# Modulation products of a two-block transformer kernel spread anew over its stages; two small elementwise steps moved from VectorE to ScalarE

## The chip, the cores and the metric

One Trainium2 chip (trn2); the kernel runs on one of its cores. The metric is device time in microseconds (us) of one execution. The kernel before took 1667.27 us, the median of three runs (1662.65 to 1669.86).

## The reference, cut to what matters

Two transformer stacks follow each other on 256 tokens of width 1024. The first has two layers (three mixing branches, a gated feed-forward, a per-layer gate). The second takes its result as `x` (the "latent" stream), has a second stream `ctx` of 256 tokens, and modulates each norm by vectors that depend on a conditioning vector alone:

```python
s_lat = silu(c); s_ctx = silu(c_ctx)
for i in range(2):                       # layer 0: pooling, layer 1: attention
    sh1, sc1, g1, sh2, sc2, g2 = split(s_lat @ ada_w[i] + ada_b[i], 6)   # 1024 -> 6 * 1024
    a_l = rms_norm(h_lat) * (1 + sc1) + sh1
    # the same with s_ctx for ctx: csh1 ... cg2 in layer 0, csh1 and csc1 alone in layer 1
    h_lat = h_lat + g1 * mixer(a_l)
    m_l = rms_norm(h_lat) * (1 + sc2) + sh2
    h_lat = h_lat + g2 * (square(relu(m_l @ mlp_w1[i])) @ mlp_w2[i])
return rms_norm(h_lat)
```

The products `s @ ada_w[i]` depend on nothing else in the program. They can be made at any time before the first use of the part concerned. In the order of their 6144 columns the parts are shift, scale, gate of the first norm, then shift, scale, gate of the second.

## The kernel before

All weights but the modulation's are read from memory once, in chunks of eight 128x128 blocks (512 KB), in an order that the function `_plan` writes out. A class `Stream` works along this list. For each chunk it issues the load into one of four `raw` buffers (L326, on SyncE's queue), makes a rounded copy `hi` on ScalarE (L368) and the remainder `lo = raw - hi` on VectorE (L377), each with five buffers. Each block is then three matmuls on TensorE: `hi` with the activations' high part (L563), `hi` with their low part (L564), `lo` with the high part (L565). A chunk is so 24 matmuls of 256 columns for one set of activations. The function `linear` runs one matrix this way: at each chunk's start it takes the next chunk and lets every background generator in `bg` make one step (`bg_step`), and after the chunk's last matmul it calls `chunk_end`.

All engines run their instructions in the order in which the Python code records them. So the place of a call in the code is the place of its instructions in each engine's queue.

The modulation matrices are 48 chunks each (`ada0`, `ada1`). `_plan` puts an `ada` chunk behind a weight chunk whenever a sum of shares (the argument `share` of `add`) reaches one. An `ada` chunk is not split. It is loaded to one of two buffers of its own, and VectorE multiplies it with the conditioning vector and sums over the row (L578, tile `aprod`): twice for the 48 chunks of `ada0` and the first 16 of `ada1` (latent and context stream), once for the other 32, so 160 products in all. `chunk_end` makes all products of an `ada` chunk at once:

```python
def ada_chunk():
    ...
    for v in range(2 if i == 0 or c < 16 else 1):
        V.scalar_tensor_tensor(out=aprod, in0=w, scalar=1.0, in1=cvec[:, v], ...)
```

When all 48 chunks are done, `mod_cols(i, c)` adds the bias and makes the gains; it is called in the feed-forward of the first stack's second layer for i = 0 and after `m101` for i = 1.

The stages, in order, are named by their weights, with the layer's number at the end. First stack: `u`, `ug`, `kr`, `fq`, `fk`, `fv` (projections), `ga`, `gc`, `uq`, `uk`, `uv`, `brc`, `bra`, `gb`, `brb` (gates and branches, with the two attentions in between), `wo`, `ff` (44 chunks), `dn`, `pl`, `pg`. Second stack: `m100`, `m200`, `m100` and `m200` again (the first half of the MLP, for context and latent), `m101` (both streams at once, so 48 matmuls to a chunk), `m201` twice, then layer 1's `k`, `v`, `q`, `awo`, `m110` to `m211`.

Three more places matter. `per_layer` (stage `pg`) takes each pair of output columns out of PSUM on VectorE (L1245), runs a tanh on ScalarE, and in a background step updates `x` on VectorE (L1250, L1251), splits it for the next layer (L707 on ScalarE, L711 on VectorE) and sums its squares for the norm (L663, L667); the next stage `u1` needs the split in its third and fourth chunks and the sums at its 22nd block (L673). `Attention.norms` scales the probabilities on VectorE (L775, L777) before TensorE transposes them (L783). `ev1` squares relu's result on VectorE (L1467).

Of the kernel before, what the change touches and what calls it, by code (L numbers as in the profile page):

```python
# [258 lines left out]
def _plan(nblocks):  # L259

    plan = []

    adas = [(f"ada{i}", c) for i in range(DEPTH) for c in range(48)]
    due = [0]

    def add(name, first=0, last=None, share=0):

        nb = nblocks[name]
        for c in range(first, -(-nb // CB) if last is None else last):
            plan.append((name, c, min(CB, nb - c * CB)))  # L270
# [18 lines left out]
    add("m200", 0, LATA, 0.3)  # L289
    add("pool")  # L290
    add("m200", LATA, None, 0.3)
    add("m100", share=0.3)
    add("m200", share=0.3)
    add("m101", share=0.9)
    for n in ("m201", "m201", "k", "v", "k"):
        add(n)
    add("q", 0, QA)
    add("v")
    add("q", QA)
    for n in ("awo", "m110", "m111", "m210", "m211"):  # L300
        add(n)
    assert not adas
    return plan

# [110 lines left out]
def body(ctx: ExitStack, tc: tile.TileContext, dram, outT):  # L415
# [156 lines left out]

    def ada_chunk():
        name, c, _ = plan[st.pos]
        i = int(name[3])
        w = st.get(name, c)
        for v in range(2 if i == 0 or c < 16 else 1):
            V.scalar_tensor_tensor(out=aprod, in0=w, scalar=1.0, in1=cvec[:, v], op0=ALU.mult, op1=ALU.mult,  # L578
                                   accum_out=ada[:, i, v, c:c + 1])
        ada_done[i] += 1  # L580
# [159 lines left out]
    class Attention:  # L740
# [520 lines left out]

    def mod_cols(i, c):

        assert ada_done[i] == 48
        used = 48 if i == 0 or c == 0 else 16
        V.tensor_tensor(out=ada[:, i, c, 0:used], in0=ada[:, i, c, 0:used], in1=pc(f"adab{i}", 0, used), op=ALU.add)
        for n in range(used // 24 if used == 48 else 1):
            sc = ada[:, i, c, 8 + 24 * n:16 + 24 * n]
            V.scalar_tensor_tensor(out=modg[:, i, c, n, :], in0=sc, scalar=1.0, in1=pc(f"ng{i}{n}"), op0=ALU.add, op1=ALU.mult)
        if i == 0:  # L1270
            V.tensor_tensor(out=gps[:, c], in0=ada[:, 0, c, 16:24], in1=pc("ps"), op=ALU.mult)
# [545 lines left out]
```

## Time and profile before

| | us |
|---|---|
| median of three runs (lowest, highest) | 1667.27 (1662.65, 1669.86) |
| the profiled execution's own time | 1675.58 |
| its span, first to last instruction | 1673.8 |
| TensorE matmuls busy in the span | 1622.0 (97%) |
| VectorE busy | 1326.3 (79%) |
| ScalarE busy | 886.7 (53%) |
| GpSimd busy | 127.0 (8%) |

Busy times are sums over the span and say nothing of a single stage. Matmuls overlap in the records, so TensorE's busy share hides short stalls; a stage's length against a like stage's shows them.

### The profile page before, as it was taken

Reading aid. Unit: us, or ns where it says so; the run is one execution under the profiler, and the core shown is the slowest. Engines: PE = TensorE matmul, PEld = TensorE weight load, DVE = VectorE, ACT = ScalarE, POOL = GpSimd, SP = SyncE. Lnnn points to the kernel's source line nnn. Section 1 sums busy time; section 2 is a strip of 40 time slices with the busy share of each in tenths; the row PEclk is TensorE's granted clock in tenths of the full one; section 3 lists DMA queues with packets and bytes.
Section 4 is the critical chain, followed back from the end, with each engine's and each line's share of the span. In section 5 each row is a group of like instructions: output and inputs, shape, how many; then the busy total and the mean of one; then the engine's idle time right before and its main releaser. Section 6 shows DMA issues by size and latency. Waiting matters only on the chain.

```text
span 1673.8 us, 32732 instructions
## 1 busy us (share of the span) xinstructions
PE 1622.0 (97%) x13326; PEld 1586.4 (95%) x13326; DVE 1326.3 (79%) x2062; ACT 886.7 (53%) x1324; POOL 127.0 (8%) x127
## 2 busy tenths in 40 slices
PE   7999999999988999999989999999999999999997
PEld 7999999999988899999989999999999999899997
DVE  7788879998989999899998789875555766776653
ACT  6665555444545455565455554653334555666643
POOL 6000100000030000011000000100000011010001
PEclk9999999999979999999999999999999999999999
DMA  7545556777756556477657666676446554155552
GB/s 262 173 161 179 172 191 227 264 256 263 265 177 214 190 182 192 165 262 232 195 191 223 230 214 215 241 246 244 160 143 202 188 173 139 51 163 188 179 196 95
DMA packets 91878, 330.72 MB, mean 198 GB/s; under 512 B 10416, under 2 KB 11088, under 8 KB 91472
## 3 DMA queue, kind: packets, MB, share of 16 engines
q1 hardware_dynamic: 89712, 322.19, 58.0%
q10 hardware_dynamic: 1440, 5.37, 0.9%
q8 instruction: 104, 1.70, 0.4%
q0 software_dynamic: 576, 1.08, 0.3%
q14 instruction: 46, 0.38, 0.1%
HBM read 326.47 MB, written 1.05 MB: 196 GB/s over the span
## 4 chain that ended last, share of the span: by engine, by line
PE 75%; DVE 16%; issue 6%; POOL 2%; ACT 1%; DMA 0%; SPq 0%; DVEq 0%; POOLq 0%; ACTq 0%
PE ps_mm L563 22%; PE ps_mm L564 22%; PE ps_mm L565 22%; DVE lo L377 6%; DVE aprod L578 2%; POOL cols L685 1%; PE sc L752 1%; PE ps_go L1667 1%; PE ps_o L793 1%; PE ps_gt L1661 0%; PE ps_l L820 0%; ACT hi L368 0%; POOL acc L663 0%; DMA x<-in_x_dram 0%; PE ps_r L690 0%
## 5 line engine op out<-in xcount | busy, mean ns | idle before, releaser
L368 ACT ACTIVATE hi<-raw 128x1024 fp32r<-128x1024 f32 x513 | 536.1, 1056 | 339.1 <-PE ps_mm L564 212.7
L377 DVE TENSOR_TENSOR lo<-raw,hi 128x1024 fp32r<-128x1024 f32 x513 | 623.4, 1233 | 57.2 <-ACT hi L368 56.4
L563 PE MATMUL ps_mm<-S1h_t,hi 128*128 128x256 f32 (+1 forms) x1456 | 414.7, 285 | 0.0
L565 PE MATMUL ps_mm<-S1h_t,lo 128*128 128x256 f32 (+1 forms) x1456 | 410.9, 282 | 2.9 <-DVE S0h_t L962 1.7
L564 PE MATMUL ps_mm<-S1l_t,hi 128*128 128x256 f32 (+1 forms) x1456 | 410.9, 282 | 1.2 <-DVE S1l_t L711 1.2
L563 PE MATMUL ps_mm<-S0h_t,hi 128*128 128x256 f32 x1200 | 339.4, 283 | 6.3 <-ACT hi L358 5.9
L565 PE MATMUL ps_mm<-S0h_t,lo 128*128 128x256 f32 x1200 | 336.3, 280 | 2.7 <-DVE lo L377 2.7
L564 PE MATMUL ps_mm<-S0l_t,hi 128*128 128x256 f32 x1200 | 335.8, 280 | 0.1
L564 PEld LDWEIGHTS ps_mm<-S1l_t,hi 128*128 128x128 f32 x1456 | 278.6, 191 | 1.8 <-DVE S1l_t L711 1.4
L565 PEld LDWEIGHTS ps_mm<-S1h_t,lo 128*128 128x128 f32 x1456 | 277.0, 190 | 3.5 <-DVE S0h_t L962 1.9
L563 PEld LDWEIGHTS ps_mm<-S1h_t,hi 128*128 128x128 f32 x1456 | 278.6, 191 | 1.1 <-issue 0.7
L563 PEld LDWEIGHTS ps_mm<-S0h_t,hi 128*128 128x128 f32 x1200 | 227.7, 190 | 7.3 <-ACT hi L358 5.9
L565 PEld LDWEIGHTS ps_mm<-S0h_t,lo 128*128 128x128 f32 x1200 | 225.9, 188 | 3.5 <-DVE lo L377 3.3
L564 PEld LDWEIGHTS ps_mm<-S0l_t,hi 128*128 128x128 f32 x1200 | 227.4, 190 | 0.4 <-DVE S0l_t L722 0.3
L578 DVE SCALAR_TENSOR_TENSOR aprod<-raw,cvec 128x1024 f32<-128x1024 f32 x160 | 195.3, 1220 | 2.2
L663 POOL TENSOR_TENSOR acc<-acc,sq 128x512 f32<-128x512 f32 x24 | 36.1, 1504 | 794.8 <-ACT sq L655 794.7
L565 PE MATMUL ps_mm<-K_t,lo 128*128 128x256 f32 x320 | 89.6, 280 | 0.2 <-DVE lo L377 0.2
L563 PE MATMUL ps_mm<-K_t,hi 128*128 128x256 f32 x320 | 89.7, 280 | 0.0
L564 PE MATMUL ps_mm<-GG_t,hi 128*128 128x256 f32 x320 | 89.5, 280 | 0.0
L565 PE MATMUL ps_mm<-VV_t,lo 128*128 128x256 f32 x288 | 80.6, 280 | 1.1 <-DVE lo L377 1.1
L563 PE MATMUL ps_mm<-VV_t,hi 128*128 128x256 f32 x288 | 80.6, 280 | 0.0
L564 PE MATMUL ps_mm<-GX_t,hi 128*128 128x256 f32 x256 | 71.8, 281 | 0.0
(429 smaller groups left out, 3024.3 us busy)
## 6 DMA issues: line engine op xcount, KB each, us to landing
raw<-in_w_m_dram SPq DMA_DIRECT2D x176, 512.0 KB, 4.3
raw<-in_w_ada_dram SPq DMA_DIRECT2D x96, 512.0 KB, 3.8
raw<-in_w_ff_dram SPq DMA_DIRECT2D x88, 512.0 KB, 4.5
raw<-in_w_dn_dram SPq DMA_DIRECT2D x44, 512.0 KB, 4.6
raw<-in_w_ga_dram SPq DMA_DIRECT2D x16, 512.0 KB, 4.3
raw<-in_w_gc_dram SPq DMA_DIRECT2D x16, 512.0 KB, 3.5
raw<-in_w_gb_dram SPq DMA_DIRECT2D x16, 512.0 KB, 4.1
raw<-in_w_wo_dram SPq DMA_DIRECT2D x16, 512.0 KB, 3.5
```

What stands on the lines that cost most here:

```text
L368: self.nc.scalar.activation(out=h[:, :n], in_=raw[:, :n], func=AF.Copy)
L377: self.nc.vector.tensor_tensor(out=l[:, :n], in0=raw[:, :n], in1=h[:, :n].bitcast(F32), op=ALU.subtract)
L563: T.matmul(ps, lhsT=wh, rhs=ah, start=first, stop=False, skip_group_check=free)
L564: T.matmul(ps, lhsT=wh, rhs=al, start=False, stop=False, skip_group_check=free)
L565: T.matmul(ps, lhsT=wl, rhs=ah, start=False, stop=last, skip_group_check=free)
L578: V.scalar_tensor_tensor(out=aprod, in0=w, scalar=1.0, in1=cvec[:, v], op0=ALU.mult, op1=ALU.mult, accum_out=ada[:, i, v, c:c + 1])
L663: e.tensor_tensor(out=self.acc[:, 0:n, :], in0=self.acc[:, 0:n, :], in1=sq[:, 0:n, :], op=ALU.add)
L685: G.tensor_tensor(out=self.cols, in0=v, in1=mhalf[:, 0:2], op=ALU.pow)
L752: T.matmul(sc[:, 0:256], lhsT=q[:, h, 128:256], rhs=k[:, h, :], start=True, stop=True)
L793: T.matmul(o[64 * e:64 * e + 64, 128 * kt:256], lhsT=self.v[:, kt, 64 * h:64 * h + 64], rhs=self.pT[e][:, 256 * kt:256 + 128 * kt], start= ...
L1667: T.matmul(o[:, 0:256], lhsT=va[:, b, (h // 2) * P:(h // 2 + 1) * P], rhs=ptT[:, b, :], start=(b == 0), stop=(b == 3))
```

## The change

Four things. `_plan` has other shares and no longer caps the sum, so `ada` chunks stand elsewhere. An `ada` chunk's two products are made at two successive chunk ends and not at one; the chunk's buffer is freed after the second. The additions of the bias and the gains are cut into parts, each just ahead of its use, so that the later chunks may come later. And two steps go from VectorE to ScalarE: the scaling of the first stack's probabilities (two instructions per head, 64 in all), and the square after relu (32).

```diff
@@ _plan
-            due[0] = min(due[0], 1) + share
-            if due[0] >= 1 and adas and (adas[0][0] == "ada0" or "ff1" in {p[0] for p in plan}):
+            due[0] += share
+            if due[0] >= 1 and adas:
...
-        for n in ("dn", "pl", "pg"):
-            add(f"{n}{i}", share=share)
+        add(f"dn{i}", 0, 16, share=(0.42, 0.1)[i])
+        add(f"dn{i}", 16)
+        for n in ("pl", "pg"):
+            add(f"{n}{i}")
...
+    add("m201", share=0.85)
+    add("m201", share=0.6)
@@ body
+    def ada_product():
+
+        at, w, vs = ada_left[0]
+        name, c, _ = plan[at]
+        i, v = int(name[3]), vs.pop(0)
+        V.scalar_tensor_tensor(out=aprod, in0=w, scalar=1.0, in1=cvec[:, v], op0=ALU.mult, op1=ALU.mult,
+                               accum_out=ada[:, i, v, c:c + 1])
+        if not vs:
+            ada_left.pop(0)
+            ada_done[i] += 1
+            st.free_ada(at)
 
     def chunk_end():
+
+        if ada_left:
+            ada_product()
         while st.next_name().startswith("ada"):
-            ada_chunk()
-            st.load_ada()
+            at = st.pos
+            name, c, _ = plan[at]
+            ada_left.append((at, st.get(name, c), [0, 1] if name == "ada0" or c < 16 else [0]))
+            ada_product()
@@ Attention.norms
-                    V.tensor_scalar(out=pts[e][:, a:b], in0=pts[e][:, a:b], scalar1=sm[:, c:c + 1], scalar2=None, op0=ALU.mult)
+                    A.activation(out=pts[e][:, a:b], in_=pts[e][:, a:b], func=AF.Copy, scale=sm[:, c:c + 1])
@@ ev1
-                V.tensor_tensor(out=r, in0=r, in1=r, op=ALU.mult)
+                A.activation(out=r, in_=r, func=AF.Square)
```

Products at the chunk ends of each stretch, counted from the two plans (160 in each):

| stretch | before | after |
|---|---|---|
| ff0 | 34 | 36 |
| dn0, first 16 chunks | 14 | 13 |
| dn0's last six, pl0, pg0, u1, ug1 | 18 | 1 |
| kr1 to wo1 | 30 | 18 |
| ff1 | 18 | 16 |
| dn1, pl1, pg1 | 14 | 4 |
| m100, m200 (first runs) | 9 | 12 |
| m100, m200 (second runs) | 10 | 10 |
| m101 | 13 | 24 |
| m201 (first run) | 0 | 14 |
| m201 (second run) | 0 | 9 |
| k | 0 | 1 |
| m110 | 0 | 2 |

On VectorE, from the second pair's `x` update in `pg0` to the fourth and last pair's read of PSUM (`PP_t` is the pair's working tile, `S1l_t` the low part of the next layer's input), the queue before reads:

```order
L1251 TENSOR_TENSOR x<-x,PP_t 128x512
L578 SCALAR_TENSOR_TENSOR aprod,ada<-raw,cvec 128x1024 x2
L377 TENSOR_TENSOR lo<-raw,hi 128x1024
L711 SCALAR_TENSOR_TENSOR S1l_t<-x,par,S1h_t 128x256 x4
L1245 TENSOR_TENSOR PP_t<-ps_mm,row 128x512
L377 TENSOR_TENSOR lo<-raw,hi 128x1024
L1250 SCALAR_TENSOR_TENSOR PP_t<-PP_t,Q_t 128x512
L1251 TENSOR_TENSOR x<-x,PP_t 128x512
L578 SCALAR_TENSOR_TENSOR aprod,ada<-raw,cvec 128x1024 x2
L711 SCALAR_TENSOR_TENSOR S1l_t<-x,par,S1h_t 128x256 x2
L1245 TENSOR_TENSOR PP_t<-ps_mm,row 128x512
```

The same stretch of the changed kernel's VectorE queue:

```order
L1270 TENSOR_TENSOR x<-x,PP_t 128x512
L386 TENSOR_TENSOR lo<-raw,hi 128x1024
L730 SCALAR_TENSOR_TENSOR S1l_t<-x,par,S1h_t 128x256 x4
L1264 TENSOR_TENSOR PP_t<-ps_mm,row 128x512
L386 TENSOR_TENSOR lo<-raw,hi 128x1024
L1269 SCALAR_TENSOR_TENSOR PP_t<-PP_t,Q_t 128x512
L1270 TENSOR_TENSOR x<-x,PP_t 128x512
L730 SCALAR_TENSOR_TENSOR S1l_t<-x,par,S1h_t 128x256 x2
L1264 TENSOR_TENSOR PP_t<-ps_mm,row 128x512
```

Four products that stood ahead of the last pair's read of PSUM are gone from the queue, and nothing else moved.

On VectorE, from the last outputs of `kr1` (`GX_t` and `P_t` are its outputs, `CQ_t` their split) to the first read of `fq1` out of PSUM (`Q_t`), the queue before reads:

```order
L711 SCALAR_TENSOR_TENSOR CQ_t<-P_t,par,CQ_t 128x256 x2
L578 SCALAR_TENSOR_TENSOR aprod,ada<-raw,cvec 128x1024 x2
L377 TENSOR_TENSOR lo<-raw,hi 128x1024
L1012 TENSOR_TENSOR GX_t<-ps_mm,row 128x512
L1017 SCALAR_TENSOR_TENSOR CQ_t<-GX_t,par,CQ_t 128x256 x3
L1021 TENSOR_TENSOR acc<-acc 128x256
L1022 TENSOR_TENSOR acc<-acc,sq 128x256
L377 TENSOR_TENSOR lo<-raw,hi 128x1024
L578 SCALAR_TENSOR_TENSOR aprod,ada<-raw,cvec 128x1024 x2
L377 TENSOR_TENSOR lo<-raw,hi 128x1024
L881 COPY PP_t<-ps_f 128x16
L924 TENSOR_TENSOR Q_t<-ps_mm,row 64x2x256 x2
```

The same stretch of the changed kernel's VectorE queue:

```order
L730 SCALAR_TENSOR_TENSOR CQ_t<-P_t,par,CQ_t 128x256 x2
L386 TENSOR_TENSOR lo<-raw,hi 128x1024
L1031 TENSOR_TENSOR GX_t<-ps_mm,row 128x512
L1036 SCALAR_TENSOR_TENSOR CQ_t<-GX_t,par,CQ_t 128x256 x3
L1040 TENSOR_TENSOR acc<-acc 128x256
L1041 TENSOR_TENSOR acc<-acc,sq 128x256
L386 TENSOR_TENSOR lo<-raw,hi 128x1024 x2
L900 COPY PP_t<-ps_f 128x16
L386 TENSOR_TENSOR lo<-raw,hi 128x1024
L943 TENSOR_TENSOR Q_t<-ps_mm,row 64x2x256 x2
```

Here too four products left the queue ahead of the read of PSUM. Two single ones now stand earlier in `kr1`, after its second and third chunks, where the queue before had two after the first.

On VectorE in the first run of `m201`, around the reads of its context outputs out of PSUM (`CQ_t` holds the context stream), the queue before reads:

```order
L377 TENSOR_TENSOR lo<-raw,hi 128x1024 x6
L1479 SCALAR_TENSOR_TENSOR CQ_t<-ps_mm,ada,CQ_t 128x256 x4
L377 TENSOR_TENSOR lo<-raw,hi 128x1024 x4
L1479 SCALAR_TENSOR_TENSOR CQ_t<-ps_mm,ada,CQ_t 128x256 x2
L377 TENSOR_TENSOR lo<-raw,hi 128x1024 x3
```

The same place in the changed kernel:

```order
L1507 SCALAR_TENSOR_TENSOR CQ_t<-ps_mm,ada,CQ_t 128x256 x4
L589 SCALAR_TENSOR_TENSOR aprod,ada<-raw,cvec 128x1024
L386 TENSOR_TENSOR lo<-raw,hi 128x1024
L589 SCALAR_TENSOR_TENSOR aprod,ada<-raw,cvec 128x1024
L386 TENSOR_TENSOR lo<-raw,hi 128x1024 x2
L589 SCALAR_TENSOR_TENSOR aprod,ada<-raw,cvec 128x1024
L386 TENSOR_TENSOR lo<-raw,hi 128x1024
L1507 SCALAR_TENSOR_TENSOR CQ_t<-ps_mm,ada,CQ_t 128x256 x2
```

A product now stands behind nearly every `lo` of this stretch, where there was none. Each of them needs an `ada` chunk that is loaded in time.

## Rows read from the trace of the kernel before

**Rows 1.** The page: the span; granted TensorE clock in 40 slices.

```profile
span 1673.8 us, 32732 instructions
...
PEclk9999999999979999999999999999999999999999
```

**Rows 2.** Windows: length; busy PE, PEld, DVE, ACT, POOL; clock; DMA share, GB/s.

```profile
23.07:34.38 11.31, 11.31 (x99) 11.31 (x97) 10.90 (x17) 7.00 (x11) 10.55 (x19) 1.00 0.65 217
468.67:492.85 24.18, 17.98 (x104) 17.00 (x103) 20.03 (x30) 10.30 (x15) 7.06 (x6) 0.67 0.53 172
23.07:251.68 228.61, 228.14 (x1858) 219.98 (x1857) 188.56 (x328) 137.09 (x243) 31.90 (x48) 1.00 0.55 183
492.85:737.26 244.41, 231.85 (x1857) 221.20 (x1857) 224.35 (x392) 133.08 (x237) 18.51 (x19) 0.98 0.59 194
51.56:66.34 14.78, 14.78 (x115) 14.18 (x113) 9.97 (x20) 11.63 (x21) 0.00 (x0) 1.00 0.54 179
521.45:542.95 21.50, 17.03 (x114) 15.75 (x113) 18.47 (x34) 12.67 (x22) 0.00 (x0) 0.92 0.63 213
...
570.94:600.68 29.74, 27.47 (x232) 26.40 (x230) 29.15 (x60) 14.96 (x40) 0.00 (x0) 1.00 0.50 167
```

**Rows 3.** Waits of PE in 430 to 500: total us, times, longest.

```profile
PE ps_r L690 <- POOL cols L685: 2.0, 2, 1.5
PE ps_n L673 <- DVE acc L667: 1.7, 1, 1.7
```

**Rows 4.** Waits of PE in 500 to 600.

```profile
PE ps_l L820 <- DVE Q_t L924: 3.3, 1, 3.3
PE ps_t L783 <- DVE smx L775: 2.2, 1, 2.2
```

**Rows 5.** Waits of PE in 600 to 720.

```profile
PE ps_t L783 <- DVE smx L775: 1.8, 1, 1.8
```

**Rows 6.** Timeline of DVE, 440 to 496: start, us, what.

```profile
458.59 1.22 DVE L377 TENSOR_TENSOR lo<-raw,hi 128x1024 fp32r<-128x1024 f32 x1
...
462.38 1.22 DVE L578 SCALAR_TENSOR_TENSOR aprod<-raw,cvec 128x1024 f32<-128x1024 f32 x1
...
475.88 0.68 DVE L1245 TENSOR_TENSOR PP_t<-ps_mm,row 128x512 f32<-128x512 f32 x1
...
483.38 0.42 DVE L667 TENSOR_TENSOR acc<-acc 128x256 f32<-128x256 f32 x1
```

**Rows 7.** A window at the lower clock, columns as in rows 2.

```profile
476.77:493.84 17.07, 12.88 (x57) 12.29 (x58) 12.75 (x20) 8.20 (x11) 6.08 (x6) 0.50 0.56 183
```

**Rows 8.** Groups by form: count, busy us, mean ns of one, idle before.

```profile
L578 DVE SCALAR_TENSOR_TENSOR aprod<-raw,cvec 128x1024 f32<-128x1024 f32 x160 | 195.3, 1220 | 2.2
L1467 DVE TENSOR_TENSOR P_t<-P_t 128x512 f32<-128x512 f32 x32 | 21.4, 690 | 54.6 <-ACT P_t L1466 54.6
L777 DVE TENSOR_SCALAR PP_t<-PP_t,smx 128x256 f32<-128x256 f32 x32 | 13.4, 418 | 1.1
...
L767 ACT ACTIVATE PP_t<-sc,mx 128x256 f32<-128x256 f32 x32 | 15.2, 475 | 49.9 <-DVE mx L762 49.8
...
L1717 ACT ACTIVATE P_t<-P_t 128x512 f32<-128x512 f32 x16 | 10.1, 633 | 0.5
```

**Rows 9.** Windows: ff0; first m100; the two runs of m201; columns as in rows 2.

```profile
251.68:377.37 125.69, 125.21 (x1064) 125.02 (x1063) 119.57 (x160) 61.68 (x72) 1.62 (x1) 1.00 0.75 249
970.88:1017.31 46.43, 46.43 (x398) 46.43 (x398) 41.58 (x69) 27.96 (x39) 2.33 (x2) 1.00 0.70 231
1253.58:1298.80 45.22, 45.22 (x386) 45.22 (x385) 25.49 (x31) 20.27 (x23) 2.96 (x2) 1.00 0.59 187
1298.80:1343.24 44.44, 44.44 (x393) 44.44 (x391) 31.08 (x39) 24.28 (x33) 3.66 (x3) 1.00 0.60 197
```

**Rows 10.** DMA in 1072 to 1163: GB/s in 40 slices; ada loads, median us to landing.

```profile
GB/s 267 54 322 301 366 349 43 257 328 256 256 41 281 313 225 252 312 286 169 212 238 70 268 292 315 387 382 376 229 218 27 167 301 312 331 52 153 270 340 367
...
raw<-in_w_ada_dram SPq DMA_DIRECT2D x10, 512.0 KB, 5.3
```

More of the change, by code (lines that the diff above doesn't have):

```diff
@@ L276, in _plan @@
     for i in range(DEPTH):
-        for n in ("u", "ug", "kr", "fq", "fk", "fv"):
-            add(f"{n}{i}", share=0.4 * i)
+        add(f"u{i}")
+        for n in ("ug", "kr", "fq", "fk", "fv"):
+            add(f"{n}{i}", share=0.14 * i)
         for n in ("ga", "gc", "uq", "uk", "uv", "brc", "bra", "gb", "brb", "wo"):
-            add(f"{n}{i}", share=0.17 * i)
-        share = 0.4 - 0.2 * i
+            add(f"{n}{i}", share=0.12 * i)
+        share = (0.42, 0.2)[i]
         add(f"ff{i}", 0, FFB, share)
@@ L285, in _plan @@
         add(f"ff{i}", FFB, None, share)
-        for n in ("dn", "pl", "pg"):
-            add(f"{n}{i}", share=share)
+        add(f"dn{i}", 0, 16, share=(0.42, 0.1)[i])
+        add(f"dn{i}", 16)
+        for n in ("pl", "pg"):
+            add(f"{n}{i}")
     add("m100", share=0.3)
-    add("m200", 0, LATA, 0.3)
+    add("m200", 0, LATA)
     add("pool")
[L291 to L296, printed above, removed]
+    add("m200", LATA, None, 0.15)
+    add("m100", share=0.15)
+    add("m200", share=0.15)
+    add("m101", share=0.95)
+    add("m201", share=0.85)
+    add("m201", share=0.6)
+    for n in ("k", "v", "k"):
+        add(n, share=0.1)
     add("q", 0, QA)
@@ L299, in _plan @@
     add("q", QA)
-    for n in ("awo", "m110", "m111", "m210", "m211"):
+    add("awo")
+    for n in ("m110", "m111"):
+        add(n, share=0.3)
+    for n in ("m210", "m211"):
         add(n)
@@ L571, in body @@
     ada_done = [0, 0]
[L573 to L580, printed above, removed]
+    ada_left = []
+    def ada_product():
[8 more added lines that the diff above has]
+            st.free_ada(at)
     def chunk_end():
+        if ada_left:
+            ada_product()
         while st.next_name().startswith("ada"):
-            ada_chunk()
-            st.load_ada()
+            at = st.pos
+            name, c, _ = plan[at]
+            ada_left.append((at, st.get(name, c), [0, 1] if name == "ada0" or c < 16 else [0]))
+            ada_product()
     def linear(name, kt, nm, sets, evac, mid=None, group=2, late=(19, 25)):
@@ L1260, in body, with ada_ready, mod_cols, gate_cols @@
     fs = cp.tile([P, 4], F32, name="fs")
[L1262 to L1270, printed above, removed]
+    def ada_ready(i, c, a, b):
+        while ada_left:
+            ada_product()
+        assert ada_done[i] >= b, (i, b, ada_done)
+        V.tensor_tensor(out=ada[:, i, c, a:b], in0=ada[:, i, c, a:b], in1=pc(f"adab{i}", a, b), op=ALU.add)
+    def mod_cols(i, c, n):
+        ada_ready(i, c, 24 * n, 24 * n + 16)
+        sc = ada[:, i, c, 24 * n + 8:24 * n + 16]
+        V.scalar_tensor_tensor(out=modg[:, i, c, n, :], in0=sc, scalar=1.0, in1=pc(f"ng{i}{n}"), op0=ALU.add, op1=ALU.mult)
+    def gate_cols(i, c, n):
+        ada_ready(i, c, 24 * n + 16, 24 * n + 24)
+        if i == 0 and n == 0:
             V.tensor_tensor(out=gps[:, c], in0=ada[:, 0, c, 16:24], in1=pc("ps"), op=ALU.mult)
@@ L1385, in ctx_mod @@
             yield from normed(nctx2)
+            for c in range(2):
+                mod_cols(0, c, 1)
             kept["m"] = new_set(0)
@@ L1490, in body @@
     _run(linear("m100", 8, 16, sets((ch, cl)), ev1((0,), 0)))
+    for c in range(2):
+        gate_cols(0, c, 1)
     m200 = linear("m200", 16, 8, many(*hid[0, 0]), ev2((0,), None))
@@ L1671, in body @@
     fl = {}
+    gate_cols(1, 0, 0)
+    mod_cols(1, 0, 1)
     def ev_ao(j, banks):
```

11 lines of the change are left out of this document (7 added, 4 removed).

## The prediction

> **What bounds the kernel now.** I read the page first: the span is 1673.8 us, and TensorE's granted clock is at 0.9 or more in all 40 slices but one, the twelfth, which is at 0.7 [rows 1]. The clock has two levels, 2.4 and 1.2 GHz, so something happens there. TensorE is the bound, and a stall is found by comparing a stage with its like. I cut the trace at the first matmul of each stage, counted in program order (24 matmuls to a chunk), and set the first stack's two layers side by side. The four chunks of `ug0` take 11.31 us with TensorE never idle, the four of `u1` 24.18. From `ug0` to `wo0` the first layer takes 228.61 us, the same work in the second layer 244.41. Within that, `fq0` takes 14.78 and `fq1` 21.50 [rows 2]. The matmuls are the same; the visible difference is that the second layer carries modulation products on VectorE, and VectorE is busy 224.35 us there against 188.56 [rows 2].
>
> Then the waits. In 430 to 500 TensorE waits for VectorE and for GpSimd's norm step [rows 3], later twice for the probabilities (2.2 and 1.8 us) and once 3.3 us for VectorE to empty a bank [rows 4, 5]. The timeline of VectorE shows why `u1` stalls. TensorE has finished `pg0` at 468.67 us. VectorE reads the last pair out of PSUM at 475.88, because it has worked without a gap since 458.59, four products among that work [rows 6]. From that read to the norm's sum (L667, done at 483.38 + 0.42 = 483.8) it is another 7.9 us. The lower clock stands right behind this stall: 17.07 us at 0.50, from 476.77 on [rows 7]. So stalls and clock together make `u1` 12.9 us too long (24.18 - 11.31), and the rest of layer 1's mixing 15.8 (244.41 - 228.61).
>
> **The change, part by part.** A product costs 1.22 us and 0.08 to read its sum, less some overlap; I count 1.25 [rows 6, 8].
>
> *Products out of `dn0` to `ug1`.* The four ahead of the last pair's read are gone, 5.0 us. VectorE was busy throughout, so the read comes at about 470.9, 2.2 after TensorE is done. The norm's sum follows 7.9 later at 478.8. TensorE wants it at block 22 of 32, that is at 468.67 + 22/32 x 11.31 = 476.4. There remain a wait of 2.4 us, and about 0.5 for GpSimd's step behind it (two such waits were 2.0 in total, one 1.5, so the other 0.5 [rows 3]). `u1` then takes 14.2, a gain of 10.0, provided the clock stays up. Of the two ends, the upper is 12 (only the 0.5 and little else remain). For the lower, the clock falls as now: TensorE's work in those 17.07 us filled 12.88 [rows 7], at twice the pace it would need 6.4 less, so the gain is 10.0 - 6.4 = 3.6. I take 10, since the stall shrinks from several pieces close together to one of 2.4, and in `ga1` (570.94 to 600.68) TensorE waited 2.2 us [rows 4] with the clock at 1.00 throughout [rows 2].
>
> *Products in `kr1` to `wo1`: 30 become 18, one at a time.* Four go from between `kr1`'s outputs and the first read of `fq1`. In `fq1` all 6.7 us (21.50 - 14.78) are then open to be saved; two products come earlier in `kr1` and delay the same queue by perhaps 1.2, so I take 4.5. The other 9.1 of the 15.8 hold the waits for the probabilities, a little lower clock (0.98 [rows 2]) and small waits. The pair of products ahead of `ga1`'s second turn is gone; elsewhere singles remain. I take 5.5 of 9.1. Together 10, with ends at 5 (half) and 14 (all but the sums that the remaining 18 products leave).
>
> *Scaling of probabilities on ScalarE.* The nearest rows are the exponentials there, 0.475 us for 128x256, against 0.418 for the scaling on VectorE [rows 8]. I take this 0.06 for each of the four instructions of a pair of heads: 0.23 us more on the path to the transposes. TensorE waited for it at two of sixteen places [rows 4, 5]; I charge 0.5 in all. If all sixteen were exposed it would be 3.7. At the same time VectorE is relieved, which is already in the 5.5.
>
> *Square on ScalarE.* 0.633 there against 0.690 on VectorE [rows 8], 32 times. It follows a relu on the same engine, so one hand-over less. ScalarE is 60% busy or less in these stages (27.96 of 46.43 in the first `m100`, [rows 9]); nothing on the path.
> The Trainium skill speaks against both moves: its page "ScalarE: Activation LUTs", section "Rules for kernel authors", says to use VectorE and not ScalarE for relu, add and multiply. These rows do not bear it out for the square (0.633 against 0.690), and for the scaling only by a tenth.
>
> *The places that receive products.* First `m100`: six more, eight squares fewer: 41.58 + 6 x 1.25 - 8 x 0.69 = 43.6 of 46.43 us. `ff0`: two more, 119.57 + 2.5 = 122.1 of 125.69. As it is, `ff0` runs at 95% VectorE with TensorE busy 125.21 of 125.69 [rows 9], so such shares are covered: zero, with ends at 2.0 and 2.5 if all that is added were exposed. `m101` has two streams to a chunk and VectorE half idle: zero. `m201` is the new load. In its first run VectorE goes from 25.49 to 25.49 + 14 x 1.25 = 43.0 of 45.22, in the second from 31.08 to 31.08 + 9 x 1.25 = 42.3 of 44.44 [rows 9]. That is 95% too, with the same cover: `lo` is made up to four chunks ahead (2.83 us each), so about 8.5 us of lateness hide.
>
> But each product also needs its `ada` chunk. The first run then loads 16 + 14 chunks of 0.524 MB, 15.7 MB in 45.22 us, 348 GB/s. The trace shows 249 GB/s at a share of 0.75 in `ff0`, which is 332 at full time [rows 9], and slices of 387 [rows 10]. At 332 the loads would take 47.4, 2.2 too long, within the cover of four `raw` buffers.
> The Trainium skill's page "DMA: Bandwidth & Descriptors", section "Specifications", gives a core about 358 GB/s from its memory; by that the loads would take 43.9 us and just fit, and no stretch here holds such a rate for 45 us.
>
> The two `ada` buffers are tighter: a load is issued when a product frees a buffer and lands 5.3 us later in a stretch with much traffic [rows 10], so two products need 5.3 + 1.25 = 6.55 us where two chunks last 5.65. That is 0.45 too slow per product, 6.3 over 14, less two chunk ends without a product (5.65). I charge 1, ends 0 and 6.
>
> **The sum.** -10 - 10 + 0.5 + 1 = -18.5 us. The profiled execution took 1675.58, 1.8 us around its span; it would take 1657.1. It stands 8.3 above the median of the runs shown, so I subtract the same 18.5 from the median: 1667.27 - 18.5 = about **1649 us**. Measurement tells about 0.5% (8.3 us) from no change.
>
> **The rivals.** *The clock falls anyway.* The remaining 2.4 us in `u1` suffice, and the gain there is 3.6 in place of 10: about 1655. For it: a fall follows the stalls in `u1`, and clocks below one appear in `fq1` too (0.92 [rows 2]). Against it: the full clock through the 2.2 us wait in `ga1`. 20%.
>
> *The delay only moves.* VectorE does the same 160 products, and the attention's chain, now over two engines, gives back what `kr1` to `wo1` gains, by the 3.7 of an exposed ScalarE and up to 5 of products that sit at new bad places: 1658 to 1663. What ScalarE's part of it would be is the 3.7 above, 1652 with all else as forecast.
> It is what the rule of the Trainium skill's page "ScalarE: Activation LUTs" would lead to, by which these steps belong on VectorE.
>  Against it: only two of sixteen turns waited. 8%.
>
> *Loads in `m201` bound VectorE, and the kernel is slower.* Every product of the 23 waits for its chunk, then the `lo` behind it, then TensorE. With a landing L each product needs (L + 1.25)/2 against 2.83 us. To eat 18.5 + 1 charged back and the 8.5 of cover, about 27 us over 23 products, it needs 1.2 us each, L = 6.8; to be slower by 0.5%, 36/23 = 1.55 each, L = 7.5. At L = 8 it is 41 - 8.5 over 1648: about 1681. The median is 5.3 in the fullest stretch before. 4% for slower; 7% for a middle case (L near 6: 18 - 8.5, so 1657 to 1660).
>
> **How the numbers follow.** The forecast as summed has 61%, with its own range 1638 to 1654 (u1 gain 8 to 12, mixing 7 to 14, m201 0 to 3). The clock rival lies at 1650 to 1659. The range to 1660 takes these in and half of the middle case; above it are the moved delay and the slower case. Below 1637 both upper ends would have to be met and more. Faster by over 0.5% (under 1659): 61 + 20 + half of the middle and moved cases, 0.87. Within: 0.09. Slower: 0.04.
>
> **What would show it.** `u1` at 12 to 15 us in place of 24.18; no stretch of 17 us at the lower clock behind it; one wait of about 2.4 us for the norm's sum at most. `fq1` within 2 us of 14.78 and no 3.3 us wait at `ps_l`. No wait of 2 us at `ps_t`; where one stays, ScalarE is named as its releaser. In `m201` VectorE near 95% and TensorE without gaps, with a length near 45.2 and 44.4; idle time ahead of the products there, ended by an `ada` load, would show the last rival. I am wrong if `u1` keeps its length with the products gone: then its stall was not VectorE's queue. I am wrong too if the stages before `u1` or after `m100` grow by what `u1` gives.

## The result and the profile after

The changed kernel takes 1642.45 us (median of four runs, 1638.20 to 1650.68) against 1666.19 for the kernel before (four runs). The ratio is 0.9868 with a 95% interval of 0.9834 to 0.9902, so it is faster by 16.3 to 27.7 us. Two more comparisons of the same two kernels gave 0.9863 (0.9827 to 0.9898) and 0.9850 (0.9807 to 0.9894). The forecast was 1649, with a range from 1637 to 1660.

The profiled execution of the changed kernel has a span of 1639.2 us, 34.6 less than that of before [rows 1]. That is more than the medians differ by; the last section accounts for the larger part of the surplus. The page's first line and its row of the granted clock:

```profile
span 1639.2 us, 32781 instructions
...
PEclk9999999999999999999999999999999999999999
```

The twelfth slice, which stood at 0.7, is full now. In the listing of the changed kernel the lines stand lower: `lo` is made in L386 (L377 before), the product is L589 (L578), the norm's sum L686 (L667), `cols` L704 (L685). Cut at the first matmul of each stage, as in the prediction, these are windows of the changed kernel, columns as in rows 2: `u1`; from `ug1` to `wo1`; `fq1`; `ga1`; `bra1`; the two runs of `m201`.

```profile
470.27:485.75 15.48, 13.62 (x104) 13.13 (x103) 12.63 (x18) 8.73 (x13) 5.55 (x5) 0.89 0.51 170
485.75:714.71 228.96, 228.11 (x1859) 219.70 (x1858) 195.42 (x326) 144.65 (x269) 19.75 (x20) 1.00 0.57 188
514.15:528.71 14.56, 14.56 (x115) 14.14 (x113) 10.92 (x21) 11.65 (x21) 0.00 (x0) 1.00 0.54 182
555.15:582.60 27.45, 27.45 (x231) 26.79 (x230) 25.11 (x49) 20.25 (x51) 0.00 (x0) 1.00 0.50 157
638.88:652.87 13.99, 13.99 (x122) 13.44 (x121) 9.90 (x19) 9.62 (x25) 4.06 (x3) 1.00 0.43 132
...
1217.46:1260.98 43.52, 43.52 (x386) 43.52 (x385) 37.02 (x47) 21.49 (x25) 2.96 (x2) 1.00 0.83 293
1260.98:1308.89 47.91, 45.95 (x392) 45.58 (x391) 43.36 (x62) 24.35 (x33) 4.58 (x3) 1.00 0.88 309
```

`u1` fell from 24.18 to 15.48. Layer 1's mixing fell from 244.41 to 228.96 [rows 2], which is layer 0's 228.61 within half a microsecond. `fq1` stands at 14.56 (21.50 before), `ga1` at 27.45 (29.74), and in none of the three mixing stages is TensorE idle. The waits of TensorE, from 430 to 500, then from 495 to 600, from 600 to 715, and in the two runs of `m201`:

```profile
PE ps_n L692 <- DVE acc L686: 1.9, 1, 1.9
PE ps_r L709 <- POOL cols L704: 0.4, 1, 0.4
...
PE ps_r L709 <- ACT row L711: 0.5, 1, 0.5
...
PE ps_mm L573 <- DVE S1l_t L743: 0.3, 1, 0.3
...
PE ps_r L709 <- POOL cols L704: 2.0, 1, 2.0
```

The waits for the probabilities and for the bank `ps_l` [rows 4, 5] are gone. One wait is new: 2.0 us in the second run of `m201`, where the kernel before had none.

In `u1` the timeline of VectorE has the last pair read out of PSUM at 472.27, 2.0 us after TensorE has left `pg0` at 470.27 (7.2 before [rows 6]), and the norm's sum at 479.63:

```profile
472.27 0.68 DVE L1264 TENSOR_TENSOR PP_t<-ps_mm,row 128x512 f32<-128x512 f32 x1
...
479.63 0.42 DVE L686 TENSOR_TENSOR acc<-acc 128x256 f32<-128x256 f32 x1
```

So the read comes 2.0 late (2.2 forecast), the sum 7.8 behind it (7.9), and TensorE waits 1.9 and 0.4 (2.4 and 0.5). What the forecast had put to a rival is the clock. It falls here too, but for a short stretch, 3.4 us of which this is a part:

```profile
481.20:484.30 3.10, 3.10 (x15) 2.80 (x15) 2.33 (x3) 1.39 (x2) 2.86 (x3) 0.50 0.62 209
```

In it ten matmuls start 213 ns apart, which at full clock take 113 to 118; that costs 1.0 us. Together 11.31 + 1.9 + 0.4 + 1.0 = 14.6 of the 15.48. The rest is for the greater part the norm's own work on TensorE: `u1` has six small matmuls for the sums and the row (L692, L709) that `ug0`, which the 11.31 is from, has not. Their price shows in the run `early` (see the experiments), where the clock stays at 1.00 through all of `u1`:

```profile
462.64:476.99 14.35, 12.42 (x104) 12.02 (x103) 12.20 (x18) 8.73 (x13) 4.84 (x5) 1.00 0.49 160
...
PE ps_n L692 <- DVE acc L686: 1.1, 1, 1.1
PE ps_r L709 <- POOL cols L704: 0.8, 1, 0.8
```

14.35 less 11.31, 1.1 and 0.8 leaves 1.1 us, for which the forecast had no term.

### The profile page after: what moved, and what is told of

Same layout as the page of the kernel before. It is cut to its first block, busy times and chain, and to the rows that moved or that the text cites. A ratio compares the mean times of both kernels' runs of the same rounds, so it can differ in the third digit from the quotient of the medians.

```text
span 1639.2 us, 32781 instructions
## 1 busy us (share of the span) xinstructions
PE 1604.8 (98%) x13326; PEld 1571.7 (96%) x13326; DVE 1287.5 (79%) x1975; ACT 928.5 (57%) x1420; POOL 129.1 (8%) x127
## 4 chain that ended last, share of the span: by engine, by line
PE 81%; DVE 9%; issue 6%; POOL 1%; ACT 1%; DMA 1%; SPq 0%; DVEq 0%; POOLq 0%; ACTq 0%
PE ps_mm L572 24%; PE ps_mm L573 24%; PE ps_mm L574 24%; DVE lo L386 4%; POOL cols L704 1%; DVE aprod L589 1%; PE sc L771 1%; PE ps_o L812 1%; PE ps_go L1697 1%; PE ps_w L1073 1%; PE ps_w L1071 1%; PE ps_w L1072 1%; DMA raw<-in_w_fq_dram 1%; PE ps_r L709 0%; PE sc L772 0%
## 5 line engine op out<-in xcount | busy, mean ns | idle before, releaser
L377 ACT ACTIVATE hi<-raw 128x1024 fp32r<-128x1024 f32 x513 | 535.6, 1055 | 318.9 <-PE ps_mm L573 196.1
L386 DVE TENSOR_TENSOR lo<-raw,hi 128x1024 fp32r<-128x1024 f32 x513 | 627.6, 1237 | 77.9 <-ACT hi L377 76.9
L572 PEld LDWEIGHTS ps_mm<-S1h_t,hi 128*128 128x128 f32 x1456 | 274.9, 189 | 1.1 <-issue 0.7
L589 DVE SCALAR_TENSOR_TENSOR aprod<-raw,cvec 128x1024 f32<-128x1024 f32 x160 | 194.8, 1218 | 6.6 <-DMA raw<-in_w_ada_dram 6.4
```

What stands on the lines that cost most here:

```text
L377: self.nc.scalar.activation(out=h[:, :n], in_=raw[:, :n], func=AF.Copy)
L386: self.nc.vector.tensor_tensor(out=l[:, :n], in0=raw[:, :n], in1=h[:, :n].bitcast(F32), op=ALU.subtract)
L572: T.matmul(ps, lhsT=wh, rhs=ah, start=first, stop=False, skip_group_check=free)
```

## The experiments

Theory 1 was that the placing of the products does everything, ScalarE's new work nothing. The rivals: that VectorE's relief by ScalarE made the attention faster (theory 2), that the clock or a late queue behind `u1` made the mixing slow, and that number or pairing of the products alone is to blame.

The table gives for each run the median, the ratio to the kernel before with its interval, and three stages of its profiled execution: `u1`, `kr1` to `wo1`, and the second run of `m201`. For the stages and the span TensorE's two paces (last section) are taken out: an interval of 113 ns between two matmuls is counted like one of 118, 4.4 ns more for each. "Share" is that of the intervals at 113 in all at either pace. `back_u1`, `two`, `mix30` and `pairs18` ran on another chip than the eight other runs of these experiments, with the kernel before beside them but not the changed one; for them the stages count more than the median.

| run | median us | ratio [95%] | u1 | kr1 to wo1 | 2nd m201 | span, one pace | share |
|---|---|---|---|---|---|---|---|
| before | 1666.19 | | 24.40 | 237.43 | 45.89 | 1691.6 | 0.35 |
| changed | 1642.45 | 0.9868 [0.9834, 0.9902] | 15.78 | 220.31 | 48.30 | 1664.8 | 0.49 |
| again | 1642.35 | 0.9863 [0.9827, 0.9898] | 16.77 | 220.51 | 50.20 | 1670.3 | 0.53 |
| again_b | 1638.91 | 0.9850 [0.9807, 0.9894] | 16.76 | 220.51 | 47.31 | 1664.3 | 0.49 |
| plan_only | 1641.45 | 0.9868 [0.9830, 0.9905] | 15.99 | 220.50 | 50.98 | 1669.6 | 0.34 |
| act_only | 1663.30 | 1.0000 [0.9973, 1.0028] | 23.27 | 237.80 | 45.90 | 1686.9 | 0.28 |
| back_u1 | 1647.74 | 0.9890 [0.9854, 0.9926] | 19.71 | 222.47 | 50.64 | 1672.8 | 0.54 |
| two | 1639.90 | 0.9834 [0.9778, 0.9889] | 18.34 | 220.51 | 49.82 | 1668.3 | 0.69 |
| pairs_u1 | 1647.19 | 0.9892 [0.9856, 0.9929] | 24.09 | 222.44 | 49.98 | 1679.9 | 0.62 |
| mix30 | 1643.88 | 0.9863 [0.9827, 0.9899] | 15.66 | 226.34 | 49.48 | 1670.0 | 0.58 |
| pairs18 | 1644.86 | 0.9881 [0.9835, 0.9928] | 15.12 | 221.29 | 50.21 | 1667.8 | 0.60 |
| pairs30 | 1653.93 | 0.9926 [0.9891, 0.9961] | 16.78 | 233.18 | 49.80 | 1681.8 | 0.55 |
| early | 1636.16 | 0.9835 [0.9807, 0.9864] | 14.38 | 220.49 | 45.90 | 1661.5 | 0.53 |
| early_b | 1632.66 | 0.9814 [0.9776, 0.9852] | 15.11 | 220.30 | 45.89 | 1661.5 | 0.65 |

**The yardstick.** The changed kernel without any edit, twice.

> The changed kernel itself once more, as the yardstick for the other runs beside it: 1642 us, 1638 to 1651 as in its four runs. In its profile u1 takes 15.5 us, kr1 to wo1 217.7, and the m201 runs show one wait of about 2 us for the norm's cols. The spans of matmuls that hold 113 ns between starts, and those that hold 118, may stand elsewhere than in the first profile: where a pause sets the pace anew, the switches lie at pauses again; if the pace belonged to the place in the program, the same chunks would have the same pace.

> The changed kernel once more, as the yardstick for the one ahead: 1642 us in the median, the second m201 run at 47.9 to 50 us.

The medians came as expected. `u1` took 16.42 and 16.43 us as profiled, one more than the first time: the second wait was 0.7 and 0.8 us (0.4 the first time), and the half clock lasted longer (mean 0.86 in both against 0.89). So one kernel's `u1` lies between 15.8 and 16.8 us at one pace, and its second run of `m201` between 47.3 and 50.2; smaller differences of these stages tell nothing.

**Which half of the change does it.** First the new spread alone, with both operations back on VectorE:

```diff
-                    A.activation(out=pts[e][:, a:b], in_=pts[e][:, a:b], func=AF.Copy, scale=sm[:, c:c + 1])
+                    V.tensor_scalar(out=pts[e][:, a:b], in0=pts[e][:, a:b], scalar1=sm[:, c:c + 1], scalar2=None, op0=ALU.mult)
...
-                A.activation(out=r, in_=r, func=AF.Square)
+                V.tensor_tensor(out=r, in0=r, in1=r, op=ALU.mult)
```

> The new spread of products with probability scaling and square back on VectorE. If the placing of the products does all (theory 1): as the changed kernel within 3 us, u1 at 15.5, kr1 to wo1 at 217.7 to 219. If the relief of VectorE in the attention by ScalarE gives a part of what kr1 to wo1 gained beyond the 10 us of the forecast (theory 2): 4 to 6 us slower than the changed kernel, kr1 to wo1 at 222 to 224, with a wait for the probabilities of about 2 us at one or two turns.

Then the same two edits the other way round, on the kernel before:

> The kernel before with only the probability scaling and the square moved to ScalarE. Theory 1: as before within 3 us, u1 at 24, kr1 to wo1 at 244, the waits for the probabilities still there, now with ScalarE as their releaser. Theory 2: 4 to 6 us faster than before, kr1 to wo1 at 238 to 240, no wait for the probabilities over 1 us. If ScalarE were the worse engine for both, as the skill's rule has it: up to 3.7 us slower.

(The 244 of these expectations counts `ug1` with the mixing; `kr1` to `wo1` alone are 233.05 us as profiled before, and 233.25 in this run.) The spread alone has the whole gain, 1641.45 against 1642.35 for the changed kernel on the same chip; the two moves alone have none, at a ratio of 1.0000. The waits of the second run, `kr1` to `wo1`, are those of before, with ScalarE as releaser where VectorE stood in [rows 4]:

```profile
PE ps_l L820 <- DVE Q_t L924: 3.4, 1, 3.4
PE ps_t L783 <- ACT PP_t L777: 2.3, 1, 2.3
```

So theory 2 falls. The scaling itself is slower on ScalarE, 0.500 us against 0.418 [rows 8] for its larger shape and 0.387 against 0.280 for the smaller (after, then before):

```profile
L796 ACT ACTIVATE PP_t<-PP_t,smx 128x256 f32<-128x256 f32 x32 | 16.0, 500 | 21.8 <-DVE smx L794 21.8
L796 ACT ACTIVATE PP_t<-PP_t,smx 128x128 f32<-128x128 f32 x32 | 12.4, 387 | 0.0
...
L777 DVE TENSOR_SCALAR PP_t<-PP_t,smx 128x128 f32<-128x128 f32 x32 | 9.0, 280 | 0.0
```

The Trainium skill's page "ScalarE: Activation LUTs", section "Rules for kernel authors", has multiplies on VectorE and not on ScalarE. These rows agree with it for the scaling, but going against it cost nothing measurable here.

**The products behind `dn0`.** 18 products go back to where they were, as singles:

```diff
-        add(f"dn{i}", 16)
+        add(f"dn{i}", 16, share=0.4 * (1 - i))
         for n in ("pl", "pg"):
-            add(f"{n}{i}")
+            add(f"{n}{i}", share=0.4 * (1 - i))
...
-        add(f"u{i}")
-        for n in ("ug", "kr", "fq", "fk", "fv"):
+        add(f"u{i}", share=0.4 * i)
+        add(f"ug{i}", share=0.4 * i)
+        for n in ("kr", "fq", "fk", "fv"):
```

> The changed kernel with 18 products put back, one to a chunk's end, into the last six chunks of dn0 and into pl0, pg0, u1 and ug1, and taken from the end of m201. If the products behind dn0 made u1 long (theory 1): u1 at 20 to 25 us in place of 15.5, a stretch of 7 to 17 us at half clock in or behind it, kr1 to wo1 still at 217 to 219, the time 5 to 9 us over the changed kernel, less the 2 to 5 that the second run of m201 gets back. If singles do no harm there and only pairs did: u1 at 15 to 17.

Only two products, in `pg0`:

```diff
+            due[0] += (name, c) == ("pg0", 4)
             if due[0] >= 1 and adas:
```

> The changed kernel with two products put back into pg0 (ends of its fifth and sixth chunk). If u1's stall is VectorE's queue, it grows by the 2.5 us of the two: TensorE waits 4 to 5 us in place of 1.9 for the norm's sum and what leads to it, u1 at 17.5 to 19 with the short fall of the clock that the changed kernel has too. If a longer stall brings the long fall (17 us at half clock, as before the change): u1 and ug1 together 4 to 6 us longer than that. If VectorE has slack there: no change of u1.

And the 18 at exactly the old places, in pairs:

```diff
+    OLD = {"dn0": (18, 20), "pl0": (1,), "pg0": (1, 4, 6), "u1": (1, 3), "ug1": (2,)}
...
+            if name in OLD and (name, c) >= ("dn0", 16):
+                due[0] += (c in OLD[name])
...
+            if ada_left and ("dn0", 16, CB) in plan[:at] and "kr1" not in {p[0] for p in plan[:at]}:
+                ada_product()
```

> The changed kernel with 18 products behind dn0's sixteenth chunk exactly where and as the kernel before has them, in pairs; put back as singles they made u1 19.7 us. If pairs make the difference to the 24.2 of before: u1 at 23 to 25 and a longer stretch at half clock behind its stall. If not: 19 to 21, and what before had above it is that run's clock. kr1 to wo1 at 217 to 219 in both.

As profiled `u1` took 18.06 with two, 19.68 with the 18 as singles and 23.86 with them in pairs, against 15.48 to 16.43 without and 24.18 before. The waits of TensorE in and around `u1` with two, and then with pairs:

```profile
PE ps_n L693 <- DVE acc L687: 2.7, 1, 2.7
PE ps_mm L575 <- DVE S0h_t L982: 1.1, 1, 1.1
PE ps_r L710 <- POOL cols L705: 0.5, 1, 0.5
```

```profile
PE ps_n L697 <- DVE acc L691: 2.3, 1, 2.3
PE ps_mm L577 <- DVE S0h_t L986: 1.7, 1, 1.7
PE ps_r L714 <- POOL cols L709: 1.5, 1, 1.5
PE ps_mm L576 <- DVE S1l_t L735: 1.2, 1, 1.2
```

Two products lengthen the waits from between 2.3 and 2.7 to 4.3 us and `u1` by 1.6 to 2.6 (18.34 against 15.78 to 16.77 at one pace), up to their own 2.5, and bring no long fall of the clock. In pairs, which also stand in `u1` itself, there are four waits close together, 6.7 us in all, and the clock is at 0.71 over the whole of `u1`:

```profile
468.98:492.84 23.86, 17.07 (x105) 16.09 (x103) 20.02 (x30) 10.30 (x15) 7.03 (x6) 0.71 0.54 181
```

This settles `u1`: its length is VectorE's queue, and the products in that queue are enough to bring it back in full. `kr1` to `wo1` stays at 222.4 in both runs with 18 products, two of the 17 us that it gained: it was not `u1`'s stall that made the mixing slow. (Most of these two stands in `fq1`, 16.55 and 16.71 us as profiled, with one wait of 0.9 at `ps_l`.)

**The products of the mixing.** More of them as singles. The text below says about 30; by the plan, and in the trace, the edit makes 26 between `kr1` and `wo1` (and one in `ug1`), eight more than the changed kernel:

```diff
-            add(f"{n}{i}", share=0.14 * i)
+            add(f"{n}{i}", share=0.25 * i)
...
-            add(f"{n}{i}", share=0.12 * i)
+            add(f"{n}{i}", share=0.17 * i)
```

> The changed kernel with about 30 products in place of 18 between u1 and ff1, still one to a chunk's end. If their number made kr1 to wo1 long before (233.1 us by its own stages against 217.6): 5 to 12 us of it come back, 223 to 230. If it was that two ran back to back, at places where the queue had no room: 217 to 220.

The 18 of the changed kernel, but two at a time:

```diff
             ada_product()
+            if ada_left and name == "ada0" and {"u1", "ff1"} & {p[0] for p in plan[:at]} == {"u1"}:
+                ada_product()
```

> The changed kernel with its 18 products between u1 and ff1 run in pairs, both at the first of their two chunk ends. If back-to-back products made kr1 to wo1 long: 222 to 230 in place of 217.6, a wait for the probabilities or at ps_l of over 1 us again. If the number or the places did: 217 to 219.

And 30 in pairs at exactly the old places:

```diff
+    OLD = {"kr1": (0, 3, 5), "fq1": (2,), "fk1": (0, 3), "fv1": (1,), "ga1": (1, 7), "gc1": (4,), "uq1": (2,), "brc1": (3,), "gb1": (1, 7), "wo1": (1,), "uk1": (), "uv1": (), "bra1": (), "brb1": ()}
...
+            if name in OLD:
+                due[0] += (c in OLD[name]) - share
...
+            if ada_left and {"u1", "ff1"} & {p[0] for p in plan[:at]} == {"u1"}:
+                ada_product()
```

> The changed kernel with the products between kr1 and wo1 exactly where and as the kernel before has them: 30, in pairs, at its chunk ends (scaling and square stay on ScalarE). 18 in pairs cost nothing there, 30 singles 4.6 us. If number and pairs act together (theory 1, refined): kr1 to wo1 at 229 to 233, all that the change gained there, and the time 11 to 16 us over the changed kernel. If the rest came from what u1's stall left behind (lower clock, a queue still late): 222 to 224, as with 30 singles.

Pairs alone cost 0.8 us at one pace (221.29 against 220.51), eight more products as singles 5.8 (226.34), twelve more, all in pairs and at the old places, 12.7 (233.18). The old waits are back, the second with ScalarE as releaser, and `fq1` is at 19.75:

```profile
PE ps_l L844 <- DVE Q_t L948: 3.1, 1, 3.1
PE ps_t L807 <- ACT PP_t L801: 2.4, 1, 2.4
```

```profile
514.25:534.00 19.75, 16.61 (x114) 15.59 (x113) 16.67 (x30) 11.73 (x21) 0.00 (x0) 0.91 0.64 213
...
497.60:726.52 228.92, 218.70 (x1762) 208.15 (x1761) 201.39 (x338) 138.13 (x261) 14.52 (x14) 0.99 0.59 194
```

In the median this is 15.0 us over the changed kernel in the same comparison (1653.93 against 1638.91). So the products at those places are enough for the greater part of what the mixing gained, 12.7 of the 17.1 us (237.43 - 220.31); 1.9 more came back with the products ahead of it in the two runs above, and about 2.5 stay open. How much is number, how much pairing and how much place is not shown: neither 30 singles nor 30 pairs elsewhere were run, and eight singles alone cost 5.8. Of the places, `fq1` has 5.1 of the 12.3 us as profiled (19.75 - 14.68 and 228.92 - 216.64, against `again_b`).

**The products of `m201`.** Most of them go into the second runs of `m100` and `m200`:

```diff
-    add("m100", share=0.15)
-    add("m200", share=0.15)
+    add("m100", share=0.5)
+    add("m200", share=0.7)
...
-    add("m201", share=0.85)
-    add("m201", share=0.6)
+    add("m201", share=0.3)
+    add("m201")
```

> The changed kernel with most products of the two m201 runs (23) moved ahead into the second runs of m100 and m200, where VectorE was busy 31.0 of 43.5 and 26.4 of 43.5 us; 5 stay in m201 and a few in k and m110. If the products in m201 are what the second run lost (a wait of 2.0 us for cols, a lo that is late for 0.2, 2.4 us in all): 2 to 3 us faster than the changed kernel, the wait gone. If that wait comes from the norms that run there and not from the products: the same time, the wait still there. If the loads now bind earlier: m100' and m200' take over 46 us together with waits of TensorE for lo, and the time is slower by what they grow.

> The kernel with most of m201's products in m100 and m200 once more, beside the changed kernel on one chip. Its second m201 run without a wait of TensorE, at 43.5 to 46 us by the pace of the matmuls, against 47.9 to 50 with the products: 3 to 5 us faster than the changed kernel in the median. If the gain of the first comparison was the pace alone: the same time.

Both times TensorE has no wait in the second run of `m201`, VectorE is busy 31.08 us there in place of 43.36, and the stage is at 45.9 us as before the change:

```profile
1251.95:1297.63 45.68, 45.68 (x393) 45.68 (x391) 31.08 (x39) 24.27 (x33) 3.65 (x3) 1.00 0.61 192
```

The receiving stages pay 0.6 and 1.0 us for it (the four runs from `m100` to the first `m201`, 226.65 and 227.09 at one pace against 226.09 in most others). The medians are 6.2 us below the changed kernel's both times (1636.16 against 1642.35, 1632.66 against 1638.91); the intervals against the kernel before still overlap. Of these 6.2 us the stages that the edit touches show about 3.7 and 0.4 in the two pairs of profiles (second run of `m201` less what the receiving stages pay); the rest stands in stages that it does not touch, or in the pace of the matmuls. By the medians this is the fastest version of the study.

## Why the forecast came out, step by step

**`u1`: -10, measured -8.7** in the first profile, -7.8 in the two others (24.18 to 15.48, 16.42 and 16.43). The mechanism holds to 0.5 us at each of its steps. Two things were left out of the sum. One is the clock: the remaining stall of 1.9 us did make it fall, as the first rival said, but for a fifth of the former 17.07 us, at a cost of 1.0. The other is the norm's own matmuls, about 1.1 us: `ug0` was taken for the like of `u1`, and has none. So `u1` came out just above the 12 to 15 us that were to show the forecast right. The argument against the rival, that the clock had stayed up through a 2.2 us wait in `ga1`, did not carry over to `u1`.

**`kr1` to `wo1`: -10, measured -15.5** (244.41 to 228.96, with `ug1`). The step that mis-sized it is "I take 5.5 of 9.1", and the 1.2 held against `fq1`. I left room for waits by the products that remain. There are hardly any: TensorE's waits in these stages are 0.5 and 0.3 us, so 18 single products lie in VectorE's idle time there (in pairs they cost 0.8), and of the 15.8 us between the layers all but 0.4 came back. `fq1` gave 6.9 (21.50 to 14.56), where 4.5 was forecast; 6.7 less the 1.2 held against it is 5.5, so 1.0 of the shortfall had no reason even in the forecast's own terms. The upper end of 14 was too low as well. At one pace the gain is larger still, 17.5 us (249.1 to 231.6, with `ug1`), since before the change more of these intervals ran at 113.

**ScalarE: +0.5, measured 0** within what can be told, by two runs from both sides. With the products gone the chain of the probabilities ends nowhere last, so that even the mis-sized instruction (0.500 us where 0.475 was taken, and 0.107 more for the smaller shape, which had no term) costs nothing.

**`m201`: +1, measured +1.4 to +5.1** (45.89 to between 47.3 and 51.0 at one pace, in the four runs whose products stand as in the changed kernel: its own three and the spread alone). The place was wrong too. The charge was for the first run, for a `lo` that comes late behind late loads; that run has no wait. The cost falls in the first chunks of the second run, where the norm's steps stand in VectorE's queue. The timeline of VectorE and then GpSimd in the changed kernel; in brackets the idle time ahead of a row and what ended it:

```profile
1262.05 1.23 DVE L589 SCALAR_TENSOR_TENSOR aprod<-raw,cvec 128x1024 f32<-128x1024 f32 x1 [1.03 <-DMA raw<-in_w_ada_dram]
...
1267.11 1.22 DVE L589 SCALAR_TENSOR_TENSOR aprod<-raw,cvec 128x1024 f32<-128x1024 f32 x1
...
1270.52 1.22 DVE L589 SCALAR_TENSOR_TENSOR aprod<-raw,cvec 128x1024 f32<-128x1024 f32 x1
...
1272.81 0.15 DVE L702 TENSOR_SCALAR nv<-ps_n 128x2 f32<-128x2 f32 x1
...
1273.04 1.61 POOL L704 TENSOR_TENSOR cols<-nv,mhalf 128x2 f32<-128x2 f32 x1 [18.65 <-DVE nv L702]
```

A product waits 1.03 us for its `ada` load, and the whole queue with it. From 1264.90 VectorE then works without a gap through two more products and several `lo` until `nv`, and TensorE waits 2.0 us for what GpSimd makes of it. In `again` and `plan_only`, the two most expensive of the four, the granted clock falls in this stage as well (0.96 and 0.97 over the run; 1.00 in the two others), and that is part of their 4.3 and 5.1. So the loads do bind a little, as the charge said, and the price is paid by a consumer that the forecast had not named. The table supports the place: the runs `back_u1` and `pairs_u1` have no product behind the fifth chunk of that run, and still show 50.6 and 50.0.

**Not in the sum: the stages from `ff1` to the second `pool`.** They carry fewer products too (10 of `dn1` became 4, the 4 of `pg1` none), and I had given them no term. TensorE's waits there, from 737 to 1075 before, were

```profile
PE ps_r L690 <- POOL cols L685: 3.3, 4, 1.8
PE ps_mm L565 <- DVE lo L377: 2.9, 4, 1.2
PE ps_p L565 <- DVE lo L377: 2.4, 1, 2.4
PE ps_p L563 <- DVE CQ_t L1338: 2.0, 1, 2.0
PE ps_p L563 <- DVE x L1338: 0.8, 1, 0.8
PE ps_p L563 <- DVE CQ_t L1479: 0.4, 1, 0.4
```

11.8 us in all; the same view of the changed kernel, 714 to 1045, adds up to 7.3, so 4.5 less. That this comes from the products of these stages was not tried by itself.

Added up, the terms miss by this much: +1.3 for `u1`, -5.5 for the mixing, -0.5 for ScalarE, +0.4 to +4.1 for `m201`, -4.5 for what was left out. From -18.5 that makes between -27.3 and -23.6; the medians have -23.7. That the whole is off by only 5.2 us is in part luck: the two terms that gave more than forecast are 10 us off one way, those that gave less 1.7 to 5.4 the other.

Against it stands a loss outside the sum: `kr0` and `fq0`, in which the change moves no product, took 34.2 us in place of 32.0, and between 31.5 and 34.4 in the other runs. Here VectorE waits for a load of constants (`cst`) that lands later, and TensorE behind it, which had no wait in these stages before (waits from 30 to 66, the kernel before and then the changed one):

```profile
DVE P_t L1003 <- DMA cst<-in_cst_dram: 2.8, 1, 2.8
...
DVE P_t L1022 <- DMA cst<-in_cst_dram: 5.1, 1, 5.1
PE ps_f L898 <- DVE GX_t L892: 0.8, 1, 0.8
PE ps_l L839 <- ACT VV_t L842: 0.7, 1, 0.7
PE ps_l L839 <- DVE Q_t L943: 0.3, 1, 0.3
```

That is not the change: `mix30`, which has it too, waits 2.2 us for `cst` and has no wait of TensorE there. What makes the load late in some executions stays open. With it the two first profiles add up at one pace: -8.6 for `u1`, -17.5 for `ug1` to `wo1`, -5.2 for `ff1` to the first run of `m200`, +2.4 for the second run of `m201` and +2.4 for `kr0` and `fq0` make -26.5 of the 26.8 us between the spans.

Of the other rivals, the moved delay did not come (no new wait in the attention), and the slower case would have needed loads that bind in `m201` throughout; its first run has no wait of TensorE, and the two runs moved 293 and 309 GB/s. One slip of the chances: 61 and 20 and half of 7 and of 8 are 88.5, not 87.

## What to carry to other kernels

Filler work on an engine that others wait for is free or dear by its place: the same 1.2 us products cost nothing in stages where that engine has slack ahead of each reader, and some 0.4 to 1.3 us each where a hand-over stands behind them in the queue. Look for the stages in which such an engine reads the last PSUM result or makes a norm's sum, keep filler out of the stretch ahead of it, and give it one piece at a time elsewhere. When work is moved, look in the receiving stage not only at busy shares but for the same kind of hand-over, as with the norm in `m201`.

## What the runs showed of the hardware

**TensorE has two paces at full clock.** The same 768 matmuls of `m101`, with TensorE never idle and the granted clock at 1.00, took 90.45 us in the profile of before and 87.04 in that of the changed kernel:

```profile
1163.12:1253.57 90.45, 90.45 (x770) 90.45 (x769) 51.42 (x72) 30.12 (x44) 0.00 (x0) 1.00 0.48 158
```

```profile
1130.42:1217.46 87.04, 87.04 (x770) 87.04 (x769) 59.09 (x87) 39.07 (x58) 0.00 (x0) 1.00 0.60 200
```

In the trace the starts of matmuls lie either 117 to 119 ns apart or 113 to 114, and hardly ever between. One pace holds until the stream of these matmuls is broken, by a wait or by other work of TensorE; behind the break it may be either. Counted as a pace where eight intervals in a row have it, there are 831 changes in the 14 profiles; 823 stand behind a break of over 150 ns, the other 8 behind an interval of at most 146 ns that was out of step. The prize can be large: `ff0` has two such breaks in its third and fourth chunk and then none that counts, and it runs at 125.69 us or, as here in a run of `early_b`, at 121.38:

```profile
253.13:374.51 121.38, 120.90 (x1064) 120.70 (x1063) 118.09 (x160) 60.87 (x72) 1.62 (x1) 1.00 0.78 258
```

`again_b` had 121.38 there as well, `again` 125.69, and these are one kernel. So the pace belongs to the execution, not to the code, at least there. How much of the spread between executions it makes differs. The profiles of `early` and `early_b`, one kernel, have spans of 1634.1 and 1628.0 us, and at one pace 1661.5 both; the three of the changed kernel, 1639.2, 1643.1 and 1639.1, do not come closer by it (1664.8, 1670.3, 1664.3). Of the 34.6 us between the two profiled spans above it is 7.7: the changed kernel has 5,777 intervals at 113 against 4,037, and 1,740 x 4.4 ns are 7.7 us. At one pace the spans differ by 26.8, and by 21.3 and 27.3 for the two other profiles of the changed kernel. What decides the pace behind a break stays open.

**The same wait may or may not pull the clock down.** Behind waits of 1.9 and 0.7 or 0.8 us in `u1` the clock fell in `again` and `again_b` (mean 0.86) and stayed at 1.00 in `pairs18` and `early_b`. Half clock is thus not decided by the length of the stall alone; the runs don't show what else does.
